# A two-layer diffusion block on one core: the last head's values earlier and its y beside other heads' w_down, one adaLN unit and GpSimd's residual rows inside the last MLP

## The chip, the cores and the metric

One core of a Trainium2 chip runs the whole kernel in one launch. The core has TensorE (PE, matrix products and transposes; its weight loads run beside them as PEld), VectorE (DVE), ScalarE (ACT), GpSimd (POOL) and SyncE (SP), whose queue here issues all loads. The metric is the device time of one execution in microseconds, the median of the runs. All times of the profile are counted from the start of its span.

## The reference, cut to what matters

256 latent tokens and 256 context tokens of width 1024 pass two layers. Layer 0 mixes with a convolution module, layer 1 with a bidirectional mLSTM of 4 heads of 512 channels; an MLP with a squared ReLU follows each. Every sub-layer is `x <- LN(ALPHA*x + gate * F(x*(1+scale)+shift))`, where shift, scale and gate are parts of `silu(c) @ w + b` (adaLN). Only the latent stream leaves the kernel, so in layer 1 the context serves as the initial state of the scan. The change lies in the end of layer 1:

```python
hsum = of[..., :INNER] * h_f + of[..., INNER:] * h_b        # of: output gate, sigmoid(xm @ w_o + b_o)
hn = (hsum - mean) * rsqrt(var + EPS) * gn_g                # per head
y = (hn + skip * xc) * silu(z)
x = LN(ALPHA * x + gate1 * (y @ w_down))
x = LN(ALPHA * x + gate2 * (square(relu(modulate(x) @ w1)) @ w2))
```

Here `h_f` and `h_b` are, for each head and direction, decayed scores times values, divided by `max(|sum of scores|, exp(-m))`.

## The kernel before, in words

*Numbers.* Everything is float32 in effect: each operand is split into a high part (a cast by ACT, L153) and the rest (a subtraction by DVE, L154), and each product is three matrix products: `mm3` (L176, L179, L180: wh·xh, wh·xl, wl·xh) and `mm3t` (L184, L185, L186) with the roles turned. Weights come by `raw_load` (L149) in blocks of 1 MB (`raw`, 3 buffers, SP's queue), and `split_w` makes two pairs `wh`, `wl` of each (4 buffers of each kind). PE needs `wh` for the first two products and `wl` for the third.

*The attention stage.* The table `att` is a list of rows [main, side, per]. Each letter is a generator: G decays, W `weights(h)`, o `gate_o(h)` (the gate by w_o, 8 blocks of weight), A `attend(h)`, D `down(h)` (y of head h times w_down, added into four accumulators for two token halves t and two column halves), E `early` (splits head 3's w_down into spare buffers ahead of time). The main chain is run step by step, and the side chain is advanced `per` steps for each (L1491 to L1500). A head's chain is W (scores times decay; POOL adds them up in `es`, L1313 and L1315; four PE products give the denominators from `es`, L1321), then A: values from memory, products into `cv`, gate (L1379), sum, statistics, norm (ACT L1393), transposes (L1401), y (DVE L1405, L1407), split. D of the last head ends with `residual` (L1471, L1472, statistics L1475).

*From w_down to the MLP.* The first weights of w1 are split early (`pre1`). `ln1(t)` for the token halves t = 0, 1: norm (L1480 to L1514), 4 transposes (L1517) for each half of the channels, scale and shift by ACT into the high part (L1521) and by DVE into a copy (L1523), and the difference of both as the low part (L1526). Between t = 0 and t = 1 stand two units of the adaLN product of the last gate (`ada_n3.mm()`, L296, 8 instructions each, weights of 2 MB each; pinned to their place among PE's pinned instructions). Then five broadcast rows of 512 KB each are loaded, and POOL scales two of them by ALPHA (L1543) and makes the residual ready, R*GA + BA (L1546). The last MLP runs in 4 chunks: `gemm` on w1 into `hid`, then w2. The first gemm takes four column groups at a time (`ko` = 4), 96 products of 256 columns, on the `pre1` weights. `gate2` adds the adaLN gate to row G2 (PE L1551) after it.

*What sets the order.* A scheduler puts the instructions of all generators into one list for each engine when the kernel is built; the order in which the code issues them is its priority. Each engine then runs its list in order, and waits where an operand isn't there.

Of the kernel before, what the change touches and what calls it, by code (L numbers as in the profile page):

```python
# [31 lines left out]
class Z:  # L32
# [11 lines left out]
    dpsum = 'mm'  # L44
    att = [['o0', 'G0 W0 W1', 2], ['o1', 'A0 W2', 1.6], ['o2', 'A1 W3 D0', 2.1], ['o3', 'A2', 1], ['D1 E3 D2', 'A3', 1.2], ['D3', '', 0]]

# [25 lines left out]
def hybrid_kernel(ctx: ExitStack, tc: tile.TileContext, xT, vecs_d, wdw_d, ada0_w, ada_w, wg_d, pw1a, pw1, pw2, w1_0, w2_0,  # L72
# [28 lines left out]
    def psum(tag="mm"):  # L101
        return pp.tile([P, 512], F32, tag=tag, name=nm(tag), bufs={"mm": 3, "ln": 2, "fl": 1, "cv": 2}[tag])
# [1178 lines left out]
    def weights(h):  # L1281
# [4 lines left out]
        for d in range(2):  # L1286
# [4 lines left out]
            for i, b in enumerate(blocks[d]):  # L1291
# [24 lines left out]
                yield  # L1316
        yield
        den = psum("ln")
        for d in range(2):
# [20 lines left out]
    def gate_o(h):  # L1340

        for d in range(2):
            bo = rows(BO().rearrange("p a b -> p (a b)"), bo_d[h:h + 1, d * DH:(d + 1) * DH])
            pss = [psum() for _ in range(2)]
            for q in range(4):
# [3 lines left out]
                for i in range(2):  # L1349
# [137 lines left out]
    def chain(names):  # L1487
        for n_ in names.split():
            yield from dict(G=decay, W=weights, o=gate_o, A=attend, D=down, E=early)[n_[0]](int(n_[1]))

# [18 lines left out]
    def ln1(t):  # L1509
# [3 lines left out]
        for g_ in range(2):  # L1513
# [5 lines left out]
            for i in range(4):  # L1519
# [5 lines left out]
                if i % 2:  # L1525
                    nc.vector.tensor_tensor(UL[f // 2][:, :, ts], y.rearrange("p (i c) -> p i c", i=4)[:, i - 1:i + 1, :],  # L1526
                                            UH[f // 2].bitcast(F32)[:, :, ts], op=ALU.subtract)
# [11 lines left out]
    HD, WX = maker(qf, "hid", 2 * DT), maker(qf, "wx", 8)  # L1539
    G2, GA, BA, GN, BN = [rows(qf.tile([P, D], F32, name=f"row{i}"), rows_d[i:i + 1]) for i in range(1, 6)]  # L1540

    for b_ in (GA, BA):
        nc.gpsimd.tensor_scalar(b_, b_, ALPHA, None, op0=ALU.mult)  # L1543
    for t in range(2):
        for b_, op in ((GA, ALU.mult), (BA, ALU.add)):
            nc.gpsimd.tensor_tensor(R[:, t, :], R[:, t, :], b_, op=op)  # L1546

# [26 lines left out]
    for c in range(4):  # L1574
# [123 lines left out]
```

## Time and profile before

| | before |
|---|---|
| time, median of 3 runs (all) | 1737.89 us (1737.48, 1737.89, 1743.78) |
| the profiled execution | 1736.14 us; span 1734.4 us, granted clock 0.993 |
| busy PE / DVE / ACT / POOL | 1694.7 / 1040.4 / 734.5 / 61.5 us |
| HBM read | 283.32 MB, 172 GB/s over the span |

A row of a timeline has start, duration, engine, line, operation, tiles, shape and count, and in brackets the idle time of that engine before it with the instruction that ended it. Durations of instructions that overlap on one engine are longer than their distance from start to start. The table of waits gives the total, the number and the longest. The granted clock is the share of full speed that PE was given.

### The profile page before, as it was taken

To read this page: it belongs to the slowest core of one execution; us is meant where nothing else is said; L and a number is where in the kernel's file an instruction comes from. 1 tells how busy PE (TensorE), PEld (TensorE's weight loads), DVE (VectorE), ACT (ScalarE), POOL (GpSimd) and SP (SyncE) were. 2 spreads that over 40 slices of the span, in tenths; PEclk is the share of its full clock that TensorE was granted. 3 is DMA by queue.
4 is the path that set the end of the run, shared out by engine and by line. 5 is a ranking of instruction groups with operands and counts; after the bars stand their busy time and mean duration, and the time that the engine had idled before them with its cause. 6 is when DMAs were issued, how large, how long until landed. Compare 5 with 4: busy or idle time off the path is not lost.

```text
span 1734.4 us, 24658 instructions
## 1 busy us (share of the span) xinstructions
PE 1694.7 (98%) x9782; PEld 1415.4 (82%) x9782; DVE 1040.4 (60%) x1846; ACT 734.5 (42%) x1161; POOL 61.5 (4%) x98
## 2 busy tenths in 40 slices
PE   8999999999999999999999999999999999989997
PEld 5655898878888999987688999998877878768996
DVE  5456895666645776762243654454487786766556
ACT  4411663231324465642333433332477564534443
POOL 0000000000000000000000000000021130030001
PEclk9999999999999999999999999999999999999999
DMA  9323524444424055568675753454445555665552
GB/s 359 140 108 130 190 74 173 150 140 146 145 98 146 25 184 172 160 204 286 239 233 162 249 167 113 156 181 169 170 171 192 190 198 188 239 225 200 191 181 91
DMA packets 69538, 300.64 MB, mean 173 GB/s; under 512 B 7026, under 2 KB 21874, under 8 KB 38704
## 3 DMA queue, kind: packets, MB, share of 16 engines
q1 hardware_dynamic: 51760, 284.39, 47.1%
q10 hardware_dynamic: 17664, 14.69, 2.5%
q8 instruction: 77, 1.26, 0.3%
q14 instruction: 37, 0.30, 0.1%
HBM read 283.32 MB, written 15.73 MB: 172 GB/s over the span
## 4 chain that ended last, share of the span: by engine, by line
PE 92%; DVE 4%; DMA 2%; ACT 1%; issue 1%; POOL 0%; SPq 0%; DVEq 0%; ACTq 0%; POOLq 0%
PE mm L176 21%; PE mm L180 20%; PE mm L179 20%; PE mm L184 3%; PE mm L185 3%; PE mm L186 3%; PE fl L296 2%; PE cv L186 2%; PE cv L185 2%; PE cv L184 2%; PE fl L697 1%; PE cv L766 1%; DMA raw<-ada_w 1%; PE ln L185 1%; PE ln L184 1%
## 5 line engine op out<-in xcount | busy, mean ns | idle before, releaser
L154 DVE TENSOR_TENSOR wl<-raw,wh 128x1024 fp32r<-128x1024 f32 x348 | 427.5, 1232 | 312.7 <-ACT wh L153 311.8
L153 ACT CAST wh<-raw 128x1024 fp32r<-128x1024 f32 x348 | 362.6, 1049 | 593.0 <-PE mm L179 385.4
L179 PE MATMUL mm<-u,wh 128*128 128x256 f32 (+1 forms) x1152 | 377.3, 328 | 0.0
L176 PE MATMUL mm<-u,wh 128*128 128x256 f32 (+1 forms) x1024 | 328.2, 322 | 6.1 <-DVE E L982 2.5
L180 PE MATMUL mm<-u,wl 128*128 128x256 f32 (+1 forms) x1024 | 326.7, 320 | 0.0
L179 PEld LDWEIGHTS mm<-u,wh 128*128 128x128 f32 x1152 | 220.6, 192 | 18.4 <-DVE mv L532 0.8
L176 PEld LDWEIGHTS mm<-u,wh 128*128 128x128 f32 x1024 | 196.1, 192 | 28.7 <-ACT wh L153 6.5
L180 PEld LDWEIGHTS mm<-u,wl 128*128 128x128 f32 x1024 | 196.4, 192 | 16.1 <-DVE wl L154 1.7
L179 PE MATMUL mm<-x,wh 128*128 128x256 f32 (+1 forms) x376 | 120.4, 320 | 3.7 <-DVE x L1526 3.7
L176 PE MATMUL mm<-xm,wh 128*128 128x512 f32 x256 | 102.9, 402 | 0.0
L184 PE MATMUL mm<-wh,xl 128*128 128x512 f32 x256 | 101.2, 396 | 0.0
L185 PE MATMUL mm<-wh,xl 128*128 128x512 f32 x256 | 100.9, 394 | 0.0
L180 PE MATMUL mm<-xm,wl 128*128 128x512 f32 x256 | 100.3, 392 | 0.0
L186 PE MATMUL mm<-wl,xl 128*128 128x512 f32 x256 | 99.6, 391 | 0.0
L176 PE MATMUL mm<-hid,wh 128*128 128x512 f32 (+1 forms) x256 | 93.3, 365 | 0.0
L180 PE MATMUL mm<-hid,wl 128*128 128x512 f32 (+1 forms) x256 | 92.8, 363 | 0.0
L179 PE MATMUL mm<-hid,wh 128*128 128x512 f32 (+1 forms) x256 | 92.8, 363 | 0.0
L372 DVE SCALAR_TENSOR_TENSOR S<-ar,cs,S 128x512 f32<-128x512 f32 x56 | 40.8, 749 | 70.0 <-DMA ar<-ada_w 69.9
L179 PEld LDWEIGHTS mm<-x,wh 128*128 128x128 f32 x376 | 71.8, 191 | 9.3 <-DVE x L1526 3.9
L179 PE MATMUL mm<-qq,wh 128*128 128x272 f32 x256 | 73.9, 289 | 0.0
L176 PE MATMUL mm<-qq,wh 128*128 128x272 f32 x256 | 73.9, 288 | 0.0
L180 PE MATMUL mm<-qq,wl 128*128 128x272 f32 x256 | 73.8, 288 | 0.0
(480 smaller groups left out, 3173.0 us busy)
## 6 DMA issues: line engine op xcount, KB each, us to landing
raw<-w SPq DMA_DIRECT2D x64, 1024.0 KB, 4.8
raw<-wo SPq DMA_DIRECT2D x32, 1024.0 KB, 4.9
raw<-ada_w SPq DMA_DIRECT2D x28, 1024.0 KB, 5.0
ar<-ada_w SPq DMA_DIRECT2D x80, 256.0 KB, 3.4
raw<-wv SPq DMA_DIRECT2D x16, 1024.0 KB, 7.3
raw<-wqT SPq DMA_DIRECT2D x16, 1024.0 KB, 5.6
raw<-wq SPq DMA_DIRECT2D x16, 1024.0 KB, 5.0
raw<-wk SPq DMA_DIRECT2D x16, 1024.0 KB, 4.9
```

The costliest lines, as they stand in the source:

```text
L153: c = nc.scalar.copy(hi, src)
L154: nc.vector.tensor_tensor(lo, src, hi.bitcast(F32), op=ALU.subtract)
L176: a = nc.tensor.matmul(ps, wh, xh, start=start, stop=False)
L179: nc.tensor.matmul(ps, wh, xl, start=False, stop=False)
L180: nc.tensor.matmul(ps, wl, xh, start=False, stop=stop)
L184: nc.tensor.matmul(ps, xh, wh, start=start, stop=False)
L185: nc.tensor.matmul(ps, xl, wh, start=False, stop=False)
L186: nc.tensor.matmul(ps, xh, wl, start=False, stop=stop)
L296: a = nc.tensor.matmul(ps[32 * j:32 * j + 32], cs[:, kt, 14 - 2 * v:46 - 2 * v], blocks[kt], start=first and kt < 4, stop=last and kt >= 4 ...
L372: nc.vector.scalar_tensor_tensor(a, w, c, a, op0=ALU.mult, op1=ALU.add)
L697: nc.tensor.matmul(wqs[0][32 * j:32 * j + 32, :], wgp[0][:, kt, :], raw[:, j * 512:(j + 1) * 512], start=kt == 0, stop=kt == ET - 1, tile_ ...
L766: return nc.tensor.matmul(o[r:r + 64, :], g_[:, r:r + 64], ps_[b][i], start=i == 0, stop=i == 1, tile_position=(0, r))
```

## The change

- `att`: a new letter V (`values(h)`) loads and splits a head's values. Head 3's V stands at the end of o3's side chain; `attend(3)` no longer loads them. Its steps per step of the main chain D1 E3 D2 go from 1.2 to 3.
- `attend(3)` issues a Sqrt activation of one element first.
- `weights` has one more `yield` before the denominators.
- The first unit of `ada_n3` stands before `ln1(0)`, the second after the first gemm of the MLP.
- The five row loads and POOL's six instructions (`rows5`) stand after that gemm, and `gate2` after the gemm of chunk 1.

```diff
-    att = [... ['o3', 'A2', 1], ['D1 E3 D2', 'A3', 1.2], ['D3', '', 0]]
+    att = [... ['o3', 'A2 V3', 1], ['D1 E3 D2', 'A3', 3], ['D3', '', 0]]
...
         yield
+        yield
         den = psum("ln")
...
+    vsp = {}
+
+    def values(h):
+        rv = raw_load(v_dr[h].rearrange("p b c -> p (b c)"))
+        vsp[h] = [split_w(rv[:, i * 1024:(i + 1) * 1024]) for i in range(2)]
+        yield
+
     def attend(h):
-        rv = raw_load(v_dr[h].rearrange("p b c -> p (b c)"))
-        vs = [split_w(rv[:, i * 1024:(i + 1) * 1024]) for i in range(2)]
-        yield
+        if h == H - 1:
+            nc.scalar.activation(con.tile([P, 1], F32, name=nm("warm")), eps, AF.Sqrt)
+        else:
+            yield from values(h)
+        vs = vsp[h]
...
+    pin[0] = True
+    ada_n3.mm()
+    pin[0] = False
     for t in range(2):
-        if t == 1:
-            pin[0] = True
-            for _ in range(2):
-                ada_n3.mm()
-            pin[0] = False
         ln1(t)
...
-    G2, GA, BA, GN, BN = [rows(qf.tile(...), rows_d[i:i + 1]) for i in range(1, 6)]
-    for b_ in (GA, BA): ...
-    for t in range(2): ...
+    G2, GA, BA, GN, BN = G5 = [qf.tile([P, D], F32, name=f"row{i}") for i in range(5)]
+    def rows5():                       # the five loads, then the same POOL instructions
+        ...
...
         if c == 0:
             acc = [[psum("ln") for _ in range(2)], [psum("cv") for _ in range(2)]]
+            rows5()
+            ada_n3.mm()
+        if c == 1:
             gate2()
```

What it does to the order, at two places. The first is DVE at the end of head 3's chain. Before (`wl_2178` and `wl_2180` are the low halves of head 2's first block of w_down, `wl_2184` and `wl_2186` of its second; `gst` and `gmv` the statistics of head 3):

```order
L154 TENSOR_TENSOR wl_2178_13497<-raw_2176_13494,wh_2177_13496 128x1024
L1384 BN_AGGR gmv_2148_13367<-gst_2147_13366 128x2
L154 TENSOR_TENSOR wl_2180_13501<-raw_2176_13494,wh_2179_13500 128x1024
L1379 SCALAR_TENSOR_TENSOR og_2100_13138<-cv_2165_13448,rden_2032_12748,og_2100_13138 128x512
L1379 SCALAR_TENSOR_TENSOR og_2132_13315<-cv_2175_13480,rden_2032_12748,og_2132_13315 128x512
L154 TENSOR_TENSOR wl_2184_13538<-raw_2182_13535,wh_2183_13537 128x1024
L1382 TENSOR_TENSOR og_2100_13138<-og_2100_13138,og_2132_13315 128x512
L154 TENSOR_TENSOR wl_2186_13542<-raw_2182_13535,wh_2185_13541 128x1024
L1383 BN_STATS gst_2147_13366<-og_2100_13138 128x6
L1384 BN_AGGR gmv_2148_13367<-gst_2147_13366 128x2
```

After (`wl_2186` and `wl_2188` are now the low halves of head 2's first block; `xl` are splits of head 3's w_down; `og_2136`, `og_2137` are y, `og_2162` the low part of y; `raw_2159` is silu(z) and skip·xc):

```order
L1416 SCALAR_TENSOR_TENSOR og_2136_13316<-ln_2160_13455,vecs_72,raw_2159_13448 128x256 x2
L1416 SCALAR_TENSOR_TENSOR og_2137_13325<-ln_2163_13479,vecs_72,raw_2159_13448 128x256
L1418 TENSOR_TENSOR og_2136_13316<-og_2136_13316,raw_2159_13448 128x512
L1416 SCALAR_TENSOR_TENSOR og_2137_13325<-ln_2163_13479,vecs_72,raw_2159_13448 128x256
L154 TENSOR_TENSOR xl_2179_13516<-raw_2175_13509,xl_2178_13515 128x512
L154 TENSOR_TENSOR og_2162_13464<-og_2136_13316,og_2161_13463 128x512
L1418 TENSOR_TENSOR og_2137_13325<-og_2137_13325,raw_2159_13448 128x512
L154 TENSOR_TENSOR xl_2181_13520<-raw_2175_13509,xl_2180_13519 128x512
L154 TENSOR_TENSOR wl_2186_13530<-raw_2184_13527,wh_2185_13529 128x1024
L154 TENSOR_TENSOR og_2165_13488<-og_2137_13325,og_2164_13487 128x512
L154 TENSOR_TENSOR xl_2183_13524<-raw_2175_13509,xl_2182_13523 128x512
L154 TENSOR_TENSOR wl_2188_13534<-raw_2184_13527,wh_2187_13533 128x1024
```

Before, both blocks of head 2's weight are split ahead of y, most of it ahead of the statistics. After, y and four splits stand ahead of the first low half.

The second is PE after the last product of w_down. Before (`res` is the residual stream that is transposed; `fl_2225` the adaLN accumulator):

```order
L1517 MATMUL ln_2221_13698<-ident_74,res_5920 128x128 x4
L1517 MATMUL ln_2223_13715<-ident_74,res_5920 128x128 x4
L296 MATMUL fl_2225_13731<-raw_2226_13732,cs_99 32x512 x4
L296 MATMUL fl_2225_13731<-raw_2227_13734,cs_99 32x512 x4
L296 MATMUL fl_2225_13731<-raw_2228_13744,cs_99 32x512 x4
L1517 MATMUL ln_2231_13762<-ident_74,res_5920 128x128 x4
L176 MATMUL mm_2235_13815<-x_2213_13686,wh_2202_13663 128x256
L176 MATMUL mm_2236_13816<-x_2213_13686,wh_2204_13667 128x256
L176 MATMUL mm_2237_13817<-x_2213_13686,wh_2207_13673 128x256
L176 MATMUL cv_2238_13818<-x_2213_13686,wh_2209_13677 128x256
L179 MATMUL mm_2235_13815<-x_2217_13690,wh_2202_13663 128x256
L180 MATMUL mm_2235_13815<-x_2213_13686,wl_2203_13664 128x256
```

After:

```order
L1528 MATMUL ln_2225_13713<-ident_74,res_5920 128x128 x4
L1528 MATMUL ln_2227_13730<-ident_74,res_5920 128x128 x4
L296 MATMUL fl_2222_13696<-raw_2223_13697,cs_99 32x512 x4
L296 MATMUL fl_2222_13696<-raw_2224_13699,cs_99 32x512 x4
L1528 MATMUL ln_2229_13750<-ident_74,res_5920 128x128 x4
L176 MATMUL mm_2233_13792<-x_2214_13688,wh_2203_13665 128x256
L176 MATMUL mm_2234_13793<-x_2214_13688,wh_2205_13669 128x256
L176 MATMUL mm_2235_13794<-x_2214_13688,wh_2208_13675 128x256
L176 MATMUL cv_2236_13795<-x_2214_13688,wh_2210_13679 128x256
L179 MATMUL mm_2233_13792<-x_2218_13692,wh_2203_13665 128x256
```

Twelve of the adaLN instructions stood between the two token halves, and the last four a little further on; now eight stand there. The other eight stand in the MLP: the first four behind the first group of products,

```order
L180 MATMUL cv_2236_13795<-x_2217_13691,wl_2211_13680 128x256
L296 MATMUL fl_2222_13696<-raw_2279_14083,cs_99 32x512
L176 MATMUL mm_2249_13920<-x_2214_13688,wh_2252_13924 128x256
L179 MATMUL mm_2249_13920<-x_2218_13692,wh_2252_13924 128x256
L296 MATMUL fl_2222_13696<-raw_2279_14083,cs_99 32x512 x3
L180 MATMUL mm_2249_13920<-x_2214_13688,wl_2253_13925 128x256
```

where the rows from `mm_2249` on belong to the next group, and the last four ahead of w2's first product. On SP the five row loads move from ahead of w1's blocks 3 and 4 to behind them (the first row to between them), and the second unit's two blocks stand behind the rows, ahead of w2's.

More of the change, by code (lines that the diff above doesn't have):

```diff
@@ L44 @@
     dpsum = 'mm'
[L45 removed]
+    att = [['o0', 'G0 W0 W1', 2], ['o1', 'A0 W2', 1.6], ['o2', 'A1 W3 D0', 2.1], ['o3', 'A2 V3', 1], ['D1 E3 D2', 'A3', 3], ['D3', '', 0]]
 _VECS = [
@@ L1488, in chain @@
         for n_ in names.split():
-            yield from dict(G=decay, W=weights, o=gate_o, A=attend, D=down, E=early)[n_[0]](int(n_[1]))
+            yield from dict(G=decay, W=weights, o=gate_o, V=values, A=attend, D=down, E=early)[n_[0]](int(n_[1]))
     for main, side, per in Z.att:
@@ L1539, in hybrid_kernel @@
     HD, WX = maker(qf, "hid", 2 * DT), maker(qf, "wx", 8)
[L1540 to L1546, printed above, removed]
+    G2, GA, BA, GN, BN = G5 = [qf.tile([P, D], F32, name=f"row{i}") for i in range(5)]
+    def rows5():
+        for i, t_ in enumerate(G5):
+            rows(t_, rows_d[i + 1:i + 2])
+        for b_ in (GA, BA):
+            nc.gpsimd.tensor_scalar(b_, b_, ALPHA, None, op0=ALU.mult)
+        for t in range(2):
+            for b_, op in ((GA, ALU.mult), (BA, ALU.add)):
+                nc.gpsimd.tensor_tensor(R[:, t, :], R[:, t, :], b_, op=op)
     def gate2():
```

## The prediction

> **What bounds the kernel now.** I read the page first, then the table of what PE waits for, then PE's own rows from the last attention head to the end of the first product group of the last MLP, and last the rows of the engines that PE waits for there. The page's engine line and its chain:
>
> ```profile
> PE 1694.7 (98%) x9782; PEld 1415.4 (82%) x9782; DVE 1040.4 (60%) x1846; ACT 734.5 (42%) x1161; POOL 61.5 (4%) x98
> ...
> PE 92%; DVE 4%; DMA 2%; ACT 1%; issue 1%; POOL 0%; SPq 0%; DVEq 0%; ACTq 0%; POOLq 0%
> ```
>
> PE is busy for 98% of the span, so no edit that leaves PE's work alone can win more than PE's gaps hold. The waits of PE from 1150 us to the end (line waited for, us in total, times, longest) show where those are:
>
> ```profile
> PE mm L179 <- DVE x L1526: 3.7, 1, 3.7
> PE ln L1517 <- DVE res L1514: 2.3, 1, 2.3
> PE ln L1321 <- POOL es L1315: 2.0, 3, 1.3
> PE mm L184 <- ACT og L153: 1.0, 1, 1.0
> ```
>
> All four are places that the change touches. PE's timeline there (start, us, operation, count, idle before and its releaser):
>
> ```profile
> 1410.12 0.61 PE L1321 MATMUL ln<-ones,es 128*128 128x1 f32 x4 [1.29 <-POOL es L1315]
> ...
> 1481.57 0.39 PE L184 MATMUL mm<-wh,og 128*128 128x512 f32 x1
> ...
> 1483.61 0.39 PE L184 MATMUL mm<-wh,og 128*128 128x512 f32 x1
> ...
> 1515.10 0.96 PE L184 MATMUL mm<-xl,og 128*128 128x512 f32 x3 [1.04 <-ACT og L153]
> ...
> 1525.92 0.39 PE L186 MATMUL fl<-xl,og 128*128 128x512 f32 x1
> 1528.63 0.63 PE L1517 MATMUL ln<-ident,res 128*128 128x128 f32 x4 [2.32 <-DVE res L1514]
> ...
> 1530.34 4.32 PE L296 MATMUL fl<-raw,cs 128*32 128x512 f32 x24
> 1534.59 0.66 PE L1517 MATMUL ln<-ident,res 128*128 128x128 f32 x4
> ...
> 1540.24 0.55 PE L179 MATMUL mm<-x,wh 128*128 128x256 f32 x1 [3.72 <-DVE x L1526]
> ...
> 1541.37 1.94 PE L296 MATMUL fl<-raw,cs 128*32 128x512 f32 x8
> 1543.24 0.87 PE L1517 MATMUL ln<-ident,res 128*128 128x128 f32 x4
> ...
> 1544.42 0.28 PE L176 MATMUL mm<-x,wh 128*128 128x256 f32 x1
> ...
> 1545.61 0.28 PE L179 MATMUL cv<-x,wh 128*128 128x256 f32 x1
> ...
> 1554.37 0.28 PE L180 MATMUL cv<-x,wl 128*128 128x256 f32 x1
> ```
>
> I call D the start of w_down of head 1 (1481.57) and T the end of issue of head 3's last product (1525.92 + 0.23 = 1526.15), so T = D + 44.6. Nine 512-column steps from 1481.57 to 1483.61 give 0.227 us each; ten 256-column steps from 1544.42 to 1545.61 give 0.119. The MLP's first product group of 96 products then needs 11.5 us, but it ends at 1554.5, T + 28.3: there most of the gaps lie. The table by windows tells a second price (busy time and count of PE, PEld, DVE, ACT, POOL, then the granted clock, DMA share, GB/s):
>
> ```profile
> 1530.00:1532.00 2.00, 2.00 (x11) 0.46 (x13) 1.96 (x7) 0.91 (x2) 0.00 (x0) 0.52 0.88 354
> 1532.00:1534.00 2.00, 2.00 (x16) 0.52 (x12) 1.44 (x4) 0.80 (x2) 0.65 (x1) 0.63 0.90 311
> 1534.00:1536.00 2.00, 1.45 (x13) 0.63 (x6) 0.23 (x1) 0.72 (x2) 2.00 (x1) 1.00 0.80 248
> ```
>
> After the idle at 1526 to 1530 PE works for 4 us at about half clock. 24 records of the adaLN unit (L296) take 4.32 us there.
>
> **The change part by part.** It concerns a stretch of 75 us and one wait ahead of it; the sum is made against the profiled execution, 1736.14 us (span 1734.4 and 1.74 around it), which is 1.75 under the median of the runs shown, 1737.89.
>
> *The second yield in weights().* The orders show that the denominators of heads 0, 1 and 2 stand at the same rows as before; only head 3's move, two PE rows (0.45 us) later, and on POOL a residual add now stands between the last two sums of es. Of the 1.29 us at 1410.12 I take 0.6 as gone (0 to 1.0).
>
> *V3 ahead, A3 three steps at a time.* The chain of head 3 (values' products, norm, y) now ends before w_down of head 2 instead of beside it. What DVE has to do there, in its order (DVE rows in timeline form; a lower-case wl or xl is the low half of a weight split at L154):
>
> ```profile
> 1511.80 0.88 DVE L1405 SCALAR_TENSOR_TENSOR og<-ln,vecs,raw 128x256 f32<-128x256 f32 x2 [0.91 <-PE ln L1401]
> 1512.71 0.69 DVE L1407 TENSOR_TENSOR og<-og,raw 128x512 f32<-128x512 f32 x1
> 1513.32 1.22 DVE L154 TENSOR_TENSOR wl<-raw,wh 128x1024 fp32r<-128x1024 f32 x1
> 1514.46 0.48 DVE L1405 SCALAR_TENSOR_TENSOR og<-ln,vecs,raw 128x256 f32<-128x256 f32 x1
> 1515.08 0.69 DVE L154 TENSOR_TENSOR og<-og,og 128x512 fp32r<-128x512 f32 x1
> ```
>
> From start to start that is 0.44 for each y half (L1405, in the new file L1416), 0.61 for L1407 (new L1418), 1.14 for a weight's low half, 0.61 for a 512-column split. ACT's casts and scaling, and the landing time of a w_down load:
>
> ```profile
> 1486.00 2.10 ACT L153 CAST wh<-raw 128x1024 fp32r<-128x1024 f32 x2
> ...
> 1509.53 1.52 ACT L1393 ACTIVATE og<-og,gmv 128x512 f32<-128x512 f32 x2
> ```
> ```profile
> raw<-wdown SPq DMA_DIRECT2D x6, 1024.0 KB, 4.8
> ```
>
> I follow the new order from D. The split of D1's second half (2 of the 4 wh/wl buffers are held by V3, as V2 holds them in the stage ahead) makes PE wait 0.4. Then 79 products of D1 and A3 run without a wait to D + 20.7, and 8 transposes to D + 21.3. The casting of head 2's weight stands on ACT behind the two scalings (1.52) and a cast, and is done at D + 21.9: 0.6 of idle. PE issues four products, to D + 22.9. The fifth needs that weight's low half, which is where the order has changed most. DVE now runs y from D + 21.25: two halves 0.88, one 0.44, L1418 0.61, one half 0.44, a split 0.61, y's split 0.61, L1418 0.61, a split 0.61, then the low half 1.14: 5.95, so D + 27.2. **PE idles 4.3 us.** Six products on, the other low half comes after two more splits and 1.14, D + 29.6: idle 1.0. The load of the second half of head 2's weight waits for the second L1418 to free its buffer (D + 25.5), lands 4.8 later and is split by D + 32.6, 0.8 before PE asks for it: hidden, but each later us beyond that would show. Together 0.4 + 0.6 + 4.3 + 1.0 = 6.3 new; the wait of 1.04 before head 3's w_down goes, and so do smaller ones before it: 193 rows at 0.227 for products, 0.6 for 8 transposes, are 42.7, so before had 1.9 of waits and after has 6.3: **+4.4**. An idle of 2.3 us with little work around it brought 4 us of half clock above; 4.3 us should too. Of the 2 us that it costs, the 1.0 wait behind it hides one. I take **+5.2** (4.0 to 6.5).
>
> The sentence of the Trainium skill that bears on this is in "TensorE: Matmul & The Clock Gate", section "Part 1: The HAM clock gate": the array falls to half rate after an idle window of about 3.4 us and needs about 3.4 us of work to come back, with a window that runs freely. By that rule a gap of 4.3 us halves the clock and costs about 1.7 us; the trace's 0.52 and 0.63 agree with the half rate, but came after a shorter idle.
>
> The Sqrt that attend(3) now issues early does not move the table load: ACT's order has it at the program's start, and the load still stands before the norm. Nothing.
>
> *adaLN unit and ln1.* t=0's two accumulators now finish ahead of t=1's, so its norm lies under head 3's products and its transposes follow T at once (before: 1528.63). Between them and the first product group stand one unit's 8 instructions (1.9 us), not 12. Also the multiply and adds of the residual rows leave POOL here:
>
> ```profile
> 1536.39 2.34 POOL L1546 TENSOR_TENSOR res<-res,row 128x1024 f32<-128x1024 f32 x1
> ...
> 1541.73 7.47 POOL L1546 TENSOR_TENSOR res<-res,row 128x1024 f32<-128x1024 f32 x3
> ```
> ```profile
> 1536.56 2.45 DVE L1526 TENSOR_TENSOR x<-S,x 128x256 fp32r<-128x256 f32 x1
> ...
> 1540.87 0.42 DVE L1526 TENSOR_TENSOR x<-S,x 128x256 fp32r<-128x256 f32 x1
> ```
>
> The DVE instruction that L179 waited for took 2.45 us while POOL's add ran, 0.42 otherwise: 2.0 of the 3.72. In the new order 19 DVE steps of t=0 and t=1 stand between T + 0.15 and that value, each 0.35 to 0.6 by the rows here, some waiting 0.46 for ACT in turn. They end at T + 7.9, so L179 at T + 8.0 instead of 1540.24 = T + 14.1. The rest of the 96 products (11.5) follows: T + 19.5 against T + 28.3, **-8.8**; half clock for a part of it, as before, takes 0 to 2.0 back. I take **-7.8**.
>
> *The second unit in the MLP.* Its 8 instructions cost on a busy PE what 16 records take at full clock:
>
> ```profile
> 267.66 1.93 PE L296 MATMUL fl<-raw,cs 128*32 128x512 f32 x16
> ```
>
> **+1.9**. Four of them fill PE's wait after the first group (0.3 + 0.5 in before): **-0.5**. Moving gate2 costs nothing by itself: same four products, between two groups. The five row loads stand on SP behind two weight loads and before the second unit's; the first load of w2 waits behind the second unit's second half. I reckon it issued at T + 23, landed at T + 28, needed at T + 30.7: hidden.
>
> *POOL's rows in the MLP.* Two scalings and four adds, 15.7 us, now start when the rows land, about T + 8, and the last three adds run from T + 16 to T + 24, across the end of the first product group, when DVE makes the low halves that PE waits for. Nothing of it is seen in before. Lower bound 0 (buffers ahead), upper bound the full 7.5. The two L1526 that ran within the three adds took 0.9 and 1.2, so I take **+1.0** (0 to 3).
>
> Sum: -0.6 + 5.2 - 7.8 + 1.9 - 0.5 + 1.0 = -0.8, so 1735.3 for the profiled execution, 1737.1 against the median. I write 1737.
>
> **The rivals.** (a) *DVE stays ahead of PE in D2.* If the wait for the low half does not show, because y starts some us earlier than I reckon, the stage loses 1.9 instead of gaining 5.2: sum -7.9, 1730.0; with the best ends of the others -10.5, 1727.4. For: A3 is stepped 2.5 times as fast. Against: the order puts nine DVE steps ahead of it. (b) *POOL and DVE lock.* If each of the three adds stops DVE for its whole length, 7.5 instead of 1.0: sum +5.7, 1743.6, slower than before; with the others' upper ends +8.6, 1746.5. It decides from the time at which the rows land: if the adds begin after T + 12 they meet the splits for certain. For: 2.45 beside 2.34. Against: 0.9 and 1.2. The Trainium skill, "SBUF — State Buffer", section "Terms", says of the port pair that DVE and GpSimd share that it is held for the full instruction and the loser fully blocks; by that rule (b) is the case, and the first of the rows above agrees. (c) *The parts do nothing.* With the D2 wait absent and no gain at ln1, +1.4 from the second unit and the yield: 1739.
>
> **How the numbers follow.** What a measurement of this kernel can tell from no change is about 0.5%, 8.7 us. My case gets 0.56 (all of it within), (a) 0.2, (b) 0.2, (c) 0.04. (a) passes -8.7 only with the other terms near their best, about half: with a little for causes that I don't see, 0.13. (b) passes +8.7 only with the others' upper ends: 0.14 with the same allowance. The range reaches to the far ends of (a) and (b): 1728 to 1746.
>
> **What would show it.** Right: PE waits of 4 and 1 us for wl L154 at D2 with a granted clock near 0.5 behind them; no wait for res before the first transposes; the first L179 some 8 us after the last w_down product; L296 in the MLP for 1.9 us; heads 0 to 2 still waiting for es. Wrong: no wait for wl at D2 (then (a)); two-input DVE splits of 2 us or more beside POOL's adds and PE waits behind them (then (b)); w2's first product waiting for its load.

## The result, and the profile after

The changed kernel takes 1740.71 us (median of 20 runs, 1736.43 to 1745.67). The kernel before, run 20 times beside it, takes 1736.40. The ratio is 1.0022 with a 95% interval of 1.0013 to 1.0032: slower, by about 3.8 us (2.3 to 5.6). The forecast was 0.8 us faster, at 1737.0. The time lies within the range given and within the 0.5% called no change, but the sign is wrong, and the interval excludes 1.

The page of the changed kernel, its engine line and chain:

```profile
span 1743.3 us, 24665 instructions
...
PE 1701.1 (98%) x9782; PEld 1419.3 (81%) x9782; DVE 1044.2 (60%) x1846; ACT 734.8 (42%) x1162; POOL 60.2 (3%) x98
...
PE 89%; DVE 5%; DMA 2%; ACT 2%; issue 1%; POOL 0%; SPq 0%; DVEq 0%; ACTq 0%; POOLq 0%
```

PE is busy 6.4 us longer than before with the same 9782 instructions, but only 1.2 of that lies behind the first w_down product of head 1 (1481.57 before, 1487.45 here), where the change does most of its work; the rest lies ahead of it. The profiled execution, 1745.03 us, is one of the longer ones of this kernel. DVE's share of the chain is 5% against 4%. The waits of PE from 1150 us to the end, as before (line waited for, us in total, times, longest):

```profile
PE mm L186 <- DVE wl L154: 3.7, 2, 3.5
PE ln L1528 <- DVE S L1534: 2.0, 1, 2.0
PE mm L180 <- DVE wl L154: 1.9, 1, 1.9
PE ln L1322 <- POOL es L1315: 1.6, 3, 0.9
PE mm L184 <- ACT wh L153: 1.4, 2, 0.9
PE mm L179 <- DVE x L1537: 1.3, 1, 1.3
```

The wait of 2.3 for res is gone, and the waits on the way to the first x low half are 2.0 and 1.3 instead of 3.7. New are 3.5 for a `wl` in head 2's w_down, and 1.9 for a `wl` in the MLP. PE's timeline at those places:

```profile
1508.87 0.87 PE L1412 MATMUL ln<-ident,og 128*128 128x128 f32 x6 [0.27 <-ACT og L1404]
1510.66 0.50 PE L184 MATMUL mm<-wh,og 128*128 128x512 f32 x1 [0.91 <-ACT wh L153]
1515.32 0.80 PE L186 MATMUL mm<-wl,og 128*128 128x512 f32 x1 [3.46 <-DVE wl L154]
...
1537.50 0.39 PE L186 MATMUL fl<-xl,og 128*128 128x512 f32 x1
1537.73 1.04 PE L1528 MATMUL ln<-ident,res 128*128 128x128 f32 x8
1538.89 1.93 PE L296 MATMUL fl<-raw,cs 128*32 128x512 f32 x16
1542.79 0.66 PE L1528 MATMUL ln<-ident,res 128*128 128x128 f32 x4 [1.98 <-DVE S L1534]
...
1546.04 0.58 PE L179 MATMUL mm<-x,wh 128*128 128x256 f32 x1 [1.31 <-DVE x L1537]
...
1566.53 0.39 PE L180 MATMUL mm<-x,wl 128*128 128x256 f32 x1 [1.92 <-DVE wl L154]
```

The first three rows are the wait at head 2 that the prediction worked out; T is 1537.50 + 0.23 = 1537.73, and the transposes follow at once. The granted clock (the third number from the end) shows what follows the waits at the two places:

```profile
1514.00:1516.00 2.00, 0.68 (x2) 0.59 (x3) 2.00 (x4) 0.23 (x1) 0.00 (x0) 0.75 0.69 197
1516.00:1518.00 2.00, 2.00 (x6) 1.53 (x5) 1.60 (x2) 0.00 (x0) 0.00 (x0) 0.50 1.12 385
...
1546.00:1548.00 2.00, 1.96 (x9) 1.96 (x10) 1.79 (x6) 0.81 (x2) 0.00 (x0) 0.50 1.01 414
```

And DVE and POOL at the end of the MLP's first product group, where PE waits 1.92:

```profile
1559.11 1.51 DVE L154 TENSOR_TENSOR wl<-raw,wh 128x1024 fp32r<-128x1024 f32 x1 [4.56 <-ACT wh L153]
1560.54 2.61 DVE L1593 TENSOR_TENSOR E<-E 128x256 f32<-128x256 f32 x1
1563.07 3.40 DVE L154 TENSOR_TENSOR wl<-raw,wh 128x1024 fp32r<-128x1024 f32 x1
1566.40 0.41 DVE L154 TENSOR_TENSOR hid<-E,hid 128x256 fp32r<-128x256 f32 x1
```
```profile
1557.15 8.24 POOL L1559 TENSOR_TENSOR res<-res,row 128x1024 f32<-128x1024 f32 x3
```

An L1593 takes 2.61 and a `wl` 3.40 while POOL's adds run; the same forms take 0.41 and 1.21 behind them.

For the comparisons below I cut the end of the program in three: D (first w_down product of head 1) to T (last product of head 3), T to KO (end of the MLP's first 96 products), and KO to the end. What lies ahead of D differs by several us from one execution to another where the order is the same (D is at 1487.5 us in the changed kernel and at 1480.7 in `latepool`, which has its order), and is left out. E, which some expectations use, is an earlier mark, 208.1 us ahead of D in the kernel before. The second last column is the change of D to end; the last is the timed ratio with its interval, from 4 to 12 runs of each version. Over these 18 kernels and the changed one the profiles' D to end lies 0.7 us below the timed difference on average, with a spread of 1.4.

| kernel | D–T | T–KO | KO–end | D–end against before | ratio |
|---|---|---|---|---|---|
| before | 44.6 | 28.3 | 179.9 | 252.8 us | |
| changed | 50.3 | 21.3 | 184.3 | +3.0 | 1.0022 [1.0013, 1.0032] |
| att | 49.9 | 24.5 | 182.8 | +4.4 | 1.0018 [1.0000, 1.0036] |
| tail | 44.6 | 25.4 | 182.6 | -0.3 | 0.9989 [0.9976, 1.0003] |
| noyield | 50.9 | 22.1 | 183.2 | +3.3 | 1.0017 [1.0003, 1.0031] |
| latepool | 51.4 | 22.1 | 183.1 | +3.8 | 1.0029 [1.0016, 1.0042] |
| poolsplit | 51.3 | 21.9 | 182.2 | +2.7 | 1.0022 [1.0009, 1.0035] |
| lateload | 50.3 | 21.4 | 186.4 | +5.2 | 1.0047 [1.0034, 1.0061] |
| units2 | 50.7 | 25.1 | 184.4 | +7.4 | 1.0054 [1.0034, 1.0075] |
| per2 | 48.8 | 22.2 | 183.2 | +1.4 | 1.0010 [0.9999, 1.0022] |
| d2first | 43.2 | 27.2 | 182.6 | +0.2 | 1.0006 [0.9993, 1.0019] |
| combo | 43.2 | 27.1 | 185.2 | +2.6 | 1.0035 [1.0022, 1.0049] |
| tailB | 44.6 | 28.3 | 180.8 | +0.9 | 1.0023 [1.0008, 1.0037] |
| tailC | 44.6 | 28.0 | 180.4 | +0.1 | 1.0009 [0.9998, 1.0021] |
| d2half | 43.2 | 29.1 | 182.1 | +1.6 | 1.0010 [0.9999, 1.0021] |
| d2half2 | 43.2 | 25.1 | 183.6 | -0.9 | 0.9999 [0.9985, 1.0013] |
| best1 | 43.2 | 27.4 | 182.2 | 0.0 | 0.9995 [0.9986, 1.0004] |
| best2 | 43.2 | 32.1 | 179.9 | +2.4 | 1.0011 [0.9998, 1.0024] |
| best3 | 43.2 | 24.1 | 183.3 | -2.2 | 0.9983 [0.9971, 0.9996] |
| tailD | 44.6 | 24.5 | 182.2 | -1.5 | 0.9998 [0.9983, 1.0013] |

### The profile page after: what moved, and what is told of

It reads as the page before. It is cut to its first block, busy times and chain, and to the rows that moved or that the text cites. A ratio compares the mean times of both kernels' runs of the same rounds, so it can differ in the third digit from the quotient of the medians.

```text
span 1743.3 us, 24665 instructions
## 1 busy us (share of the span) xinstructions
PE 1701.1 (98%) x9782; PEld 1419.3 (81%) x9782; DVE 1044.2 (60%) x1846; ACT 734.8 (42%) x1162; POOL 60.2 (3%) x98
## 4 chain that ended last, share of the span: by engine, by line
PE 89%; DVE 5%; DMA 2%; ACT 2%; issue 1%; POOL 0%; SPq 0%; DVEq 0%; ACTq 0%; POOLq 0%
PE mm L176 20%; PE mm L180 20%; PE mm L179 20%; PE mm L186 3%; PE mm L184 3%; PE mm L185 3%; PE cv L186 1%; PE cv L184 1%; PE cv L185 1%; DVE wl L154 1%; PE fl L296 1%; PE cv L766 1%; PE ln L176 1%; PE fl L697 1%; PE ln L184 1%
## 5 line engine op out<-in xcount | busy, mean ns | idle before, releaser
L179 PE MATMUL mm<-u,wh 128*128 128x256 f32 (+1 forms) x1152 | 377.7, 328 | 0.0
L179 PEld LDWEIGHTS mm<-u,wh 128*128 128x128 f32 x1152 | 220.6, 192 | 18.4 <-DVE mv L532 0.8
L179 PE MATMUL mm<-x,wh 128*128 128x256 f32 (+1 forms) x376 | 120.6, 321 | 1.3 <-DVE x L1537 1.3
L179 PE MATMUL mm<-hid,wh 128*128 128x512 f32 (+1 forms) x256 | 92.8, 363 | 0.0
L179 PEld LDWEIGHTS mm<-x,wh 128*128 128x128 f32 x376 | 72.1, 192 | 6.9 <-DVE x L1537 1.5
L179 PE MATMUL mm<-qq,wh 128*128 128x272 f32 x256 | 73.9, 289 | 0.0
```

The lines of the kernel that those rows point to most:

```text
L179: nc.tensor.matmul(ps, wh, xl, start=False, stop=False)
```

## The experiments

**The two halves of the change.** `tail` has the edits behind the attention stage alone (unit, rows, POOL, `gate2`), `att` those of the attention stage alone (V3, three steps, Sqrt). Neither has the second yield.

```diff
# tail: att table, values() and Sqrt of before
-    ['o3', 'A2 V3', 1], ['D1 E3 D2', 'A3', 3], ['D3', '', 0]
+    ['o3', 'A2', 1], ['D1 E3 D2', 'A3', 1.2], ['D3', '', 0]
# att: from ln1 on as in the kernel before
```

> The edits behind the attention stage alone (the adaLN units, the row loads and POOL's rows, gate2); the attention table, attend and weights as before. Stages: D to T (first product of head 1's w_down to the last of head 3's), T to the end of the first 96 MLP products (KO), KO to the end of the span; before 44.6, 28.3 and 179.9 us, changed 50.3, 21.3 and 184.3. Theory 1 (each term is local and they add up): D to T 44.6 as before; T to KO 23 to 24, since POOL's 2.0 and one unit at half clock leave it, but t=0's transposes still wait 2.5 after T; KO to the end 184.3; sum 0 to -1 against before. Rival (the gain at ln1 comes from the attention table's order of head 3's w_down): T to KO 27 to 28, sum +3 to +4.

> The attention edits alone (V3 ahead, A3 at 3 steps, the early Sqrt), without the extra yield; everything behind the attention stage as before. Theory 1: D to T 50.3 with waits of about 3.6 and 1.1 for head 2's weight and half clock behind; T to KO 25 to 26 (t=0's transposes at T, nothing else); KO to the end 179.9; sum +3 against before. Rival (the gain at ln1 comes from here): T to KO 21 to 22, sum -1 to -2.

Measured: `tail` leaves D to T alone, takes 2.9 from T to KO and adds 2.7 behind KO: no change or slightly faster. `att` adds 5.4 to D to T, takes 3.8 from T to KO, adds 2.9 behind KO (PE waits 1.9 for a `wl` there: POOL's adds of before now reach past KO), and is slower by its profile; its timed interval just reaches 1. So the loss is the attention edits'. In both runs T to KO lies between the ranges of the theory and of the rival, and the gain at ln1 has two sources of about the same size: -2.9 and -3.8 are about -6.8 together, and the changed kernel has -7.1. The attention edits' share comes with y, as far as the rows tell: it is early, head 3's products fill one accumulator after the other, and in the changed kernel DVE takes the first one up 7.9 us ahead of T (1529.83) instead of 5.2 (1520.98 before); in `att` it is 7.9 as well.

**The second yield.** `noyield` is the changed kernel with one yield.

```diff
         yield
-        yield
         den = psum("ln")
```

> The changed kernel without the second yield of the softmax. By the prediction the yield is worth 0.6 us (0 to 1.0), so E to D rises by 0.6 and the whole kernel by 0.6. By the waits of the changed kernel's profile (the es waits gone, a new one of 0.62 us for a high half at the next product) it is worth 0.2 or nothing, and E to D and the median stay within 0.3 us of the changed kernel's; a split block in its place at the head of PE is then on time again (no wait of 0.6).

The ratio is 1.0017 against 1.0022, no difference that the intervals can show. Its waits for es and for the high half, which are 1.6 and 1.4 in the changed kernel:

```profile
PE ln L1321 <- POOL es L1315: 2.1, 3, 1.3
...
PE mm L184 <- ACT wh L153: 0.6, 1, 0.6
```

With the second yield the waits for es are 0.5 shorter, and PE's next product waits instead, a row that neither `noyield` nor the kernel before has:

```profile
1419.06 0.50 PE L184 MATMUL mm<-wh,xl 128*128 128x512 f32 x1 [0.46 <-ACT wh L153]
```

The profiles do tell what the yield is worth. Over the same 140 records of PE's list around this place (1399.55 to 1432.53 in the changed kernel) PE takes 32.95 to 33.00 us in the nine profiles with the second yield, and 32.56 to 32.66 in ten of the eleven with one (34.24 in `best1`). So it costs about 0.35 us, ahead of D.

**POOL beside DVE.** `poolsplit` does each row add in four pieces; `lateload` moves the loads of the two rows, and POOL's work, to behind the second chunk's gemm; `latepool` moves the code of POOL's work alone to there.

```diff
# poolsplit
-                nc.gpsimd.tensor_tensor(R[:, t, :], R[:, t, :], b_, op=op)
+                for q in range(4):
+                    sl = slice(256 * q, 256 * q + 256)
+                    nc.gpsimd.tensor_tensor(R[:, t, sl], R[:, t, sl], b_[:, sl], op=op)
# latepool: the POOL loops in poolrows(), called at c == 1 ahead of gate2()
# lateload: the same, with the loads of GA and BA in poolrows() too
```

> The changed kernel with each of POOL's four adds of 1024 columns cut into four of 256. Theory (a two-input DVE instruction waits for the whole POOL instruction that runs): the DVE instructions behind the first group of the MLP that took 1.5, 2.6 and 3.4 us are held for at most one short add, 0.7 each, so none takes more than 2; PE's wait of 1.9 for wl falls to 0.5 to 1; KO to the end 183 instead of 184.3; sum -1 to -1.5 against the changed kernel. Rival (POOL and DVE share the port by turns or by bandwidth, so that only POOL's total counts): the same waits, sum 0, or more by the start of 12 further POOL instructions.

> The changed kernel with POOL's six row instructions issued after the gemm of chunk 1 instead of chunk 0; the loads stay. Theory 1 (POOL's adds hold DVE off the low halves that PE waits for behind the first group): PE's wait of 1.9 for wl there falls under 0.4, KO to the end 182 instead of 184.3, sum -2 against the changed kernel. Rival (that low half is late because its load or its place on DVE is late): the wait stays at 1.5 to 2, sum 0.

> The changed kernel with the rows GA and BA loaded, and POOL's six instructions issued, after the gemm of chunk 1: POOL has to wait for the rows, which the kernel with the late issue alone did not make it do (its POOL instructions ran at the same place as in the changed kernel). Theory (lock of POOL and DVE): the two-input DVE instructions behind the first group take 0.41 and 1.21 instead of 2.6 and 3.4, PE's wait for wl there goes from 1.9 to under 0.5, KO to the end 182 to 183 instead of 184.3. Rival (the lock only moves and costs PE the same where it meets the later splits): KO to the end 184, with a wait for wl of over 1 later.

DVE and POOL in `poolsplit`:

```profile
1555.14 1.72 DVE L154 TENSOR_TENSOR wl<-raw,wh 128x1024 fp32r<-128x1024 f32 x1 [5.01 <-ACT wh L153]
1556.78 0.95 DVE L1595 TENSOR_TENSOR E<-E 128x256 f32<-128x256 f32 x1
1557.65 1.76 DVE L154 TENSOR_TENSOR wl<-raw,wh 128x1024 fp32r<-128x1024 f32 x1
```
```profile
1551.56 12.77 POOL L1561 TENSOR_TENSOR res<-res,row 128x256 f32<-128x256 f32 x13
```

Behind the first group no DVE instruction takes more than 1.76 now, PE's wait for `wl` is gone, and KO to end is 2.1 shorter than in the changed kernel (0.9 shorter than in `latepool` and `noyield`, where the MLP is in the changed kernel's order). POOL pays for it: about 1 us for each of 13 pieces. So a DVE instruction with two inputs waits for the GpSimd instruction beside it, and the length of the GpSimd instruction sets how long. One with a single array as input doesn't: in the changed kernel, beside the add from 1551.86 to 1554.27, an L1534 took 0.41 as elsewhere, and the L1537 right behind it 1.32 instead of 0.43. The Trainium skill, "SBUF — State Buffer", section "Terms", has it as a port pair that is held for the full instruction, with the loser blocked; 3.40 beside whole rows and 1.76 beside quarters agree. The timed ratio doesn't show the gain (1.0022): D to T and T to KO came out 1.0 and 0.7 longer than in the changed kernel's profile, with the same orders there.

`latepool` tells nothing of the place: the scheduler kept POOL's work where it was (from 10.8 us after T on, against 11.3 in the changed kernel), so it is a repeat. In `lateload` the loads moved, but the three adds met the end of the first group again:

```profile
PE mm L186 <- DVE wl L154: 3.3, 1, 3.3
PE mm L180 <- DVE wl L154: 2.1, 1, 2.1
```

Its KO to end is 2.1 longer than in the changed kernel, with a granted clock of 0.50 (1563 to 1565) behind the second of these waits. It is slower than the changed kernel: moving the work by some us doesn't take it out of DVE's way.

**Both units ahead of ln1(0).**

```diff
-    ada_n3.mm()
+    for _ in range(2):
+        ada_n3.mm()
...
-            ada_n3.mm()          # in the MLP
```

> The changed kernel with both adaLN units pinned ahead of ln1(0). Theory (the gaps of 2.3, 0.7 and 1.5 us between T and the first low part of x hold a second unit for nothing): KO to the end 182.4 instead of 184.3, T to KO 21 to 22 as in the changed kernel; sum -2. Rival (its second block cannot land before T + 8, since three raw buffers are taken): T to KO 23 to 24, sum 0.

PE's waits in it:

```profile
PE mm L180 <- DVE wl L154: 3.3, 2, 2.0
PE fl L296 <- DMA raw<-ada_w: 3.0, 1, 3.0
```

The second unit's last block lands late, PE waits 3.0 for it, and T to KO is 3.9 longer. KO to end isn't shorter either, though the unit's instructions are gone from it: PE waits 2.0 and 1.3 for `wl` there. The unit's place in the MLP is worth what it costs.

**Head 2's low half ahead of y.** `per2` advances A3 by two steps instead of three. `d2first` steps A3 beside D1 D2 E3, so that D2's splits stand ahead of E3's and y.

```diff
# per2
-    ['D1 E3 D2', 'A3', 3]
+    ['D1 E3 D2', 'A3', 2]
# d2first
+    ['D1 D2 E3', 'A3', 3]
```

> The changed kernel with A3 at 2 steps instead of 3: in the order both low halves of head 2's first w_down block stand ahead of y, all else of the change stays. Theory 1: the waits of 3.5 and 0.4 for wl and the half clock behind them go, D to T 44 to 46, T to KO 21, sum -5 against the changed kernel, -1 to -2 against before. Rival (the wait only moves: y comes later and PE waits for it before head 3's products): D to T 48 to 50 with a wait for og, sum 0 to -2 against the changed kernel.

> The changed kernel with the main chain D1 D2 E3 instead of D1 E3 D2: head 2's w_down is loaded and split ahead of head 3's, so in the order its four low halves stand ahead of y. The run with 2 steps had these low halves ahead too, and PE still waited 3.4 there, for the cast, because the block itself landed late. Theory (head 2's block comes late, by DVE's order with 3 steps, by the queue of three raw buffers with 2; loading it first cures both): waits at head 2 under 0.5 in all, D to T 45 to 46 instead of 50.3, sum -4 to -5 against the changed kernel. Rival (three raw buffers are one too few as long as silu(z) holds one, whatever the order): PE waits 3 to 4 elsewhere, for xl or og ahead of head 3's products, D to T 48 to 50.

In `per2` the low halves stand ahead of y, and PE waits for the high half of the same weight instead:

```profile
1506.24 0.50 PE L184 MATMUL mm<-wh,og 128*128 128x512 f32 x1 [3.39 <-ACT wh L153]
```

D to T falls by 1.4 only. In `d2first` the wait is gone, and D to T is 43.2, 1.3 less than before. But T to KO goes back to 27.2, and the ratio is 1.0006. PE and then DVE of `d2first` around T (1524.33):

```profile
1529.61 1.08 PE L1528 MATMUL ln<-ident,res 128*128 128x128 f32 x8 [2.31 <-DVE res L1525]
```
```profile
1524.64 0.68 DVE L1482 TENSOR_TENSOR E<-fl,G 128x512 f32<-128x512 f32 x1
1525.24 0.69 DVE L1486 BATCH_NORM_STATS2 st<-res 128x6 f32<-128x512 f32 x1
1525.84 0.68 DVE L1483 TENSOR_TENSOR res<-res,E 128x512 f32<-128x512 f32 x1
1526.43 1.22 DVE L154 TENSOR_TENSOR wl<-raw,wh 128x1024 fp32r<-128x1024 f32 x1
1527.56 0.69 DVE L1486 BATCH_NORM_STATS2 st<-res 128x6 f32<-128x512 f32 x1
```

The low half in the fourth row is the last of four of w1's (1.22 us each) that stand among the residual's steps in DVE's list, and DVE runs without a gap. In the changed kernel all four are done ahead of the first step of the residual (its start 7.9 us ahead of T), and DVE still waits for PE:

```profile
1526.55 2.59 DVE L154 TENSOR_TENSOR wl<-raw,wh 128x1024 fp32r<-128x1024 f32 x2 [1.71 <-ACT wh L153]
1529.83 0.69 DVE L1482 TENSOR_TENSOR E<-mm,G 128x512 f32<-128x512 f32 x1 [0.70 <-PE mm L186]
```

Four times 1.14 from start to start are 4.6 of the 5.9 us by which T to KO is longer in `d2first`. Two tests take DVE's work out of the stretch: in `d2half` and `d2half2` the low halves of w1's blocks 2 and 3 are kept behind ln1(0), with D1 D2 E3.

```diff
# d2half2, on top of d2first
-        for m in range(2 * g_, min(2 * g_ + 2, 3 + Z.pre4)):
+    for m in range(2):                        # blocks 0 and 1 only
...
         ln1(t)
+        if t == 0:
+            for m in range(2, 3 + Z.pre4):    # their order on DVE is kept
+                pre1[m] = split_w(...)
# d2half: also keeps the order of the two normalisations of t = 0 (L1526)
```

> As d2first (head 2's low halves ahead of the next head's y), with one thing more: the low halves of w1's blocks 2 and 3 (two subtractions of 1.14 us on VectorE) are written behind the first ln1 block instead of among the residual's steps. Theory that the stretch from head 1's first w_down product to ln1 is bound by VectorE: D to T stays at 43.2 us, head 3's last product to the end of the MLP's first 96 products falls from 27.2 to 24-25.5, the end of it to the program's end stays at 182.6, so E to end 460.3-462. Rival, that what is late behind T is the adaLN unit's blocks or the transposes' own chain: 27 or over and E to end 463.

> d2half once more without its fault: there the second normalised half of the first block also stood behind the first half's whole chain, and PE waited 5.2 us for it. Here only the low halves of w1's blocks 2 and 3 (2 x 1.14 us on VectorE) stand behind the first ln1 block; the normalisations are in the order of d2first. VectorE theory: the first transposes come 2.3-3 us after T instead of 5.3, and T to the end of the MLP's first 96 products is 24-25.5 us instead of 27.2; D to T 43.2. Rival (what is late is ScalarE's chain or the loads, not VectorE): 26.5 us or over.

`d2half` failed as a test. Keeping the order of the normalisations put the second one behind the whole chain of the first half, and PE's table of waits has what that costs:

```profile
PE ln L1531 <- DVE res L1526: 5.2, 1, 5.2
```

`d2half2` doesn't do that. T is 1527.32 + 0.23 = 1527.55:

```profile
1527.32 0.39 PE L188 MATMUL fl<-xl,og 128*128 128x512 f32 x1
1528.56 1.93 PE L298 MATMUL fl<-raw,cs 128*32 128x512 f32 x16 [0.85 <-DVE E L1484]
1530.42 1.09 PE L1529 MATMUL ln<-ident,res 128*128 128x128 f32 x8
1535.16 1.12 PE L1529 MATMUL ln<-ident,res 128*128 128x128 f32 x4 [3.65 <-DVE S L1535]
```

The transposes come 2.9 after T instead of 5.3, and KO 25.1 after T instead of 27.2, for 2 x 1.14 of DVE's work moved. DVE sets the pace there, and late blocks don't: this is shown for these two. That the first two, which still stand among the residual's steps, cost as much is only argued. With the low halves moved, a wait for the second pair of transposes (3.65) is what is left.

**Versions without the wait and with split rows.** `tailB` is `tail` with the second unit back between t = 0 and t = 1, and `tailC` is `tailB` with rows in four pieces. `tailD` is `tail` with such rows. `combo` is `d2first` + `units2` + `lateload` with one yield. `best1`, `best2` and `best3` have rows in four pieces and one yield: `best1` on `d2half`, `best2` the same with both units ahead of ln1(0), `best3` on `d2half2`.

> The attention stage as before; one adaLN unit ahead of ln1(0), the other between t=0 and t=1 as before, the row loads and POOL's rows behind the first gemm as in the changed kernel, gate2 in chunk 1. Theory (a second unit on the busy PE of the MLP costs 1.9, while the run of the tail alone showed 3.8 us of idle between the two halves' transposes): D to T 44.6, T to KO 25 to 26, KO to the end 180.5 to 181; E to the end 458.5 against 460.9 before and 460.2 of the tail alone; ratio 0.998 to 0.999. Rival (the unit's blocks land late there, with three raw buffers): T to KO 27 to 28, ratio 1.000.

> The run tailB with POOL's four adds cut into four each. Theory: KO to the end 180.0, 0.5 to 1 less than tailB; ratio 0.998. Rival: as tailB, or 0.5 longer.

> tail (the attention stage as before, one yield, the second adaLN unit and GpSimd's rows in the MLP) with GpSimd's rows in four pieces each. If a VectorE instruction waits for the whole GpSimd instruction beside it, the pieces take 0.5-2 us from the 182.6 us that tail needs from the end of the 96 products to the end: 180.6-182.1, E to end 458-459.7, ratio 0.997-0.9985. If the waits of that stretch have another cause, 182.6 and tail's 0.999.

> D1 D2 E3, both units ahead of ln1(0), GA and BA and POOL's rows in chunk 1, without the extra yield. Theory: D to T 45 to 46, T to KO 21 to 22, KO to the end 180 to 181; 4 to 6 us less than before (ratio 0.997). Rival (the gaps refill each other): ratio 0.999 to 1.001.

> As d2half, with GpSimd's residual rows in four pieces of 256 columns each (no VectorE instruction then waits for a whole row) and without the second yield of the softmax. VectorE theory: D to T 43.2, T to the end of the first 96 products 24-25.5, from there to the end 181-182, E to end 457.5-460, 1733-1735 us, ratio to the kernel before 0.998-0.999. Rival (the blocks are late): 461 or over and a ratio of 1.000 or over.

> As best1, with both adaLN units ahead of the first ln1 block as in the kernel before: the only kernel here with the two changes of the attention stage's order and split GpSimd rows but no unit in the last MLP. Where the unit in the MLP costs its own 1.9 us there and nothing is gained for it ahead, E to end is 1 us lower than in best1 (457-459); where the second unit's last block lands late, as it did with both units ahead of ln1 in the changed kernel (PE 3.17 us idle), it is 2-3 us higher.

> d2half2 with GpSimd's residual rows in four pieces each and one yield in the softmax. VectorE theory: D to T 43.2, T to the end of the 96 products 24-25.5, from there to the end 181.5-182.5, E to end 457.5-460, ratio to the kernel before 0.997-0.999. Rival: T to the end of the 96 products 26.5 or over, ratio 0.9995-1.000 as best1.

`tailB`, `tailC`, `combo` and `best2` gain nothing (of the first three, 0.997 to 0.999 was expected): T to KO is 27 to 32 in all of them, in `best2` because PE waits 4.9 us for the second unit's block. `tailB` has POOL's rows in the MLP but the second unit at its old place, and its T to KO is that of before: the 2.9 of `tail` is the second unit's, and POOL's leaving and the first unit's move bring nothing together. `best1` carries `d2half`'s wait of 5.2 and ends level with the kernel before. `tailD` is 1.5 us shorter by its profile, level by its times. `best3` is the one version that comes out faster than the kernel before: 1733.80 us against 1735.11, ratio 0.9983 (0.9971 to 0.9996). With 18 versions timed, one interval that ends so close below 1 could be luck; its profile, 2.2 us shorter from D to the end, agrees with it. Its page and its PE around T (1525.36):

```profile
PE 1694.9 (98%) x9782; PEld 1415.6 (82%) x9782; DVE 1042.7 (60%) x1846; ACT 734.3 (42%) x1162; POOL 69.0 (4%) x110
```
```profile
1525.13 0.39 PE L188 MATMUL fl<-xl,og 128*128 128x512 f32 x1
1526.38 1.92 PE L298 MATMUL fl<-raw,cs 128*32 128x512 f32 x16 [0.85 <-DVE E L1483]
1528.23 1.09 PE L1528 MATMUL ln<-ident,res 128*128 128x128 f32 x8
...
1536.51 0.58 PE L181 MATMUL mm<-x,wh 128*128 128x256 f32 x1 [0.65 <-DVE x L1537]
```

PE's busy time is back at 1694.9, POOL's is 7.5 higher than before. The first product that needs an x low half starts 11.2 after T, against 14.1 before, with D to T 1.4 shorter.

## Why the prediction was wrong

Its mechanism was right in the main and its sum was not: four terms each came out on the worse side. For terms that lie in the same order in several profiles I give the mean over the changed kernel and those, and the range.

- **The second yield**, forecast -0.6: +0.35, by the stretch of 140 records given above. The wait for es falls from 1.29 to 0.86, but the next weight's high half, which that wait had covered, is 0.46 late. The step said "of the 1.29 us I take 0.6 as gone" and did not ask what is late next.
- **The D stage**, forecast +5.2 (4.0 to 6.5): +6.2, from six profiles with this order (D to T 50.3 to 51.4). The place, the instruction and the cause are those forecast: 4.3 for the first low half was 3.46, the second one of 1.0 didn't show, and 0.6 and 0.4 were 0.9 and less. What was too small is the half clock behind it. The products behind the wait take 0.43 us from start to start instead of 0.227, for so long that it costs 1.6 (changed kernel) to 3.0 us (`poolsplit`) in the six; the forecast had 2 and let the wait of 1.0 that wasn't there hide one of them. The eight transposes ahead of it took 2.5 with the waits around them in the changed kernel, not 0.6 and 0.6.
- **ln1**, forecast -7.8: -6.6 (T to KO 21.3 to 22.1 in five profiles). "L179 at T + 8.0" was 8.3. The products behind it took 13.0 instead of 11.5 + 1.0.
- **Behind KO**, forecast +2.4 (unit +1.9, fills -0.5, POOL +1.0): +4.4 in the changed kernel's profile, +3.3 and +3.2 in two others with its order. `poolsplit` parts the terms, since no wait of PE is left behind KO there: it still has +2.3, so the unit less the fills is +2.3 and not +1.4, and POOL's share is 2.1, 0.9 and 0.9, 1.3 on average instead of 1.0.

The step that failed most behind KO is the price of the unit. It was read from 16 records in one row (1.93). In the new order they stand in three groups, and these are the changed kernel's rows:

```profile
1559.08 1.04 PE L296 MATMUL fl<-raw,cs 128*32 128x512 f32 x2
...
1560.49 1.06 PE L296 MATMUL fl<-raw,cs 128*32 128x512 f32 x6
...
1575.11 1.07 PE L296 MATMUL fl<-raw,cs 128*32 128x512 f32 x8
```

From the start of each group to the next product are 0.98, 0.99 and 1.00 us, 2.97 together: a group costs 1.0 whether it has 2, 6 or 8 records. The products on both sides of a group are about 0.1 longer as well (0.21 and 0.22 from start to start instead of 0.12). That the unit's first instruction stands apart from the next three thus costs about 1.0 us, an estimate from these rows. No run keeps the four together.

POOL's +1.0 was near in size and wrong in its reason: from "the two L1526 that ran within the three adds took 0.9 and 1.2" I took a weak lock. Two instructions were too few to read it from. Behind KO a `wl` took 3.40 instead of 1.21 and an L1593 2.61 instead of 0.41, and PE waited 1.9; in `noyield` and `latepool`, whose order is the same there, a `wl` took 2.5 and the instruction behind it 2.6, and PE waited 0.4. Rival (b) named this mechanism and the condition for it (adds after T + 12) rightly; the condition held (the three adds begin 19.4 after T), and the price was 1 to 2 us, not the full 7.5. That blocks split ahead and DVE's idle time took the rest is argued, not tested.

Sum by these measures: 0.35 + 6.2 - 6.6 + 3.6 = +3.6, beside +3.8 by the times. No term failed alone: 1.0, 1.0, 1.2 and 1.2 too good make 4.4 of the 4.6 between -0.8 and +3.8.

There is a fault that the sum doesn't show. I priced the D stage (+5.2) and ln1 (-7.8) as two edits that add up. `d2first` shows that they don't come apart: both are orders of DVE's one list, and taking the wait at head 2 away gave back 5.9 of the 7.1 us at ln1, since w1's low halves then fell among the residual's steps. That a cure of one term undoes the other was not among my rivals. `d2half2` and `best3` show that it can be had without, for the most part (T to KO 25.1 and 24.1 with D to T at 43.2), and that makes the one version here that comes out faster.

Rival (a), that the wait at head 2 doesn't show, is refuted, as is (c), that the parts do nothing. The moved `gate2`, w2's first load and the Sqrt cost nothing that shows: no wait of PE names them. The first and last stand in the runs only beside the other edits.

## What to carry to other kernels

Where a second engine has no gaps over a stretch, price that stretch as one list of that engine: an instruction that is moved out of one place of it (low halves ahead of y) stands in the way at another (among the residual's steps), so a wait at the head and a gain at the tail are not two independent terms. A GpSimd instruction with two inputs that runs beside VectorE's should be costed by its length for each two-input VectorE instruction on a path, and cut in pieces if it can't be moved. Instructions that are moved should be priced in the groups in which they will stand: the adaLN unit's 16 records took 1.9 us in one row and 3.0 in three groups. When a wait is taken away, look for the next operand that the wait had been covering, and when each term of a sum rests on a friendly value, the sum is biased by all of them together.

## What the hardware showed that was not expected

- A two-input DVE instruction of 128x1024 took 1.51 and 3.40 us beside GpSimd row adds of 2.7 us (8.24 for three), 1.72 and 1.76 beside adds of a quarter row, and 1.21 alone.
- A group of the adaLN unit's records among other products costs the same for 2, 6 and 8 of them: 0.98, 0.99 and 1.00 us from its start to the next product, against 1.85 for 16 in a row (the kernel before, from 267.66 on). The code sends the four instructions of a block to different 32-column parts of the array, and the first three of the six records start within 0.02 us of each other.
- Half clock came without a single long wait. In the changed kernel PE was busy for 2.2 of the 6 us from 1540 to 1546, with waits of 1.98, 0.55 and 1.31, and the granted clock was 0.50 from 1546 to 1548. One wait of 1.85 among the MLP's products was followed by 0.50 two us later in `att` (1561 to 1563), and one of 1.92 in the changed kernel by 1.00 up to 1575, so the length of a wait alone doesn't tell. The Trainium skill, "TensorE: Matmul & The Clock Gate", section "Part 1: The HAM clock gate", speaks of a window of about 3.4 us; the wait of 3.46 at head 2 agrees with it, and no single wait at ln1 of the changed kernel is that long.
- GpSimd's adds in quarters took 12.77 us for 13 pieces, about 3.9 for a whole row, against 8.24 for 3 whole rows (2.7 each).
